# Batch norm with ReLU on one core: other roles for the two DMA queues, and stores of another size

## The chip, the cores and the metric

The kernel runs on one core of a Trainium2 chip. The metric is the device time of one execution in microseconds.

## The reference

```python
x = randn(32, 128, 32, 32)          # float32, 16.78 MB
normalized = (x - running_mean[None, :, None, None]) / sqrt(running_var[None, :, None, None] + eps)
scaled = normalized * gamma[None, :, None, None] + beta[None, :, None, None]
out = maximum(scaled, 0)            # float32, 16.78 MB
```

Per channel this is one scale, one bias and a ReLU. All 33.56 MB must pass between HBM (the memory beside the chip's cores, where the arrays lie) and SBUF (the core's own memory, on which the engines work).

## The kernel before

The 4096 (batch, channel) rows of 1024 numbers are laid out as two halves t, each of 128 partitions with 16 rows j. A row is 4 KB, and the rows of one partition are contiguous in HBM. `TILES` lists tiles as (half, first row, end row). A transfer of n rows is, for each partition, one contiguous run of n x 4 KB.

```python
TILES = ((0, 0, 2), (0, 2, 4), (0, 4, 8), (0, 8, 16), (1, 0, 16))
LOAD_CUTS = {(1, 8)}
STORE_CUTS = {(0, 1)}
HALVES = {(0, 0), (0, 1)}
# ...
for t, a, b in TILES:                                   # all loads: sync queue
    xt = data.tile([P, b - a, HW], F32, name=f"x{t}_{a}")
    cuts = [a] + [j for j in range(a + 1, b) if (t, j) in LOAD_CUTS] + [b]
    for c, d in zip(cuts, cuts[1:]):
        nc.sync.dma_start(out=xt[:, c - a : d - a, :], in_=xr[t, :, c:d, :])
# ...
for k, src in enumerate((running_var, gamma, running_mean, beta)):
    nc.scalar.dma_start(out=raw[:, k, :], in_=src.rearrange("(q j) -> q j", j=J))
# ... a matmul spreads the parameters over 128 partitions; Sqrt, reciprocal and
# ... three small VectorE operations make scale_t and bias_t
for t, a, b, xt in tiles:
    first = a
    for j in range(a, b):
        step = HW // 2 if (t, j) in HALVES else HW
        for w in range(0, HW, step):
            nc.scalar.activation(out=xt[:, j - a, w : w + step], in_=xt[:, j - a, w : w + step],
                                 func=ACTF.Relu, bias=bias_t[:, j : j + 1], scale=scale_t[:, j : j + 1])
        if j + 1 == b or (t, j + 1) in STORE_CUTS:      # all stores: scalar queue
            nc.scalar.dma_start(out=outr[t, :, first : j + 1, :], in_=xt[:, first - a : j + 1 - a, :])
            first = j + 1
```

## Time and profile before

| | before |
|---|---|
| time, median of the first 3 runs | 83.82 us (83.80 to 83.85) |
| span in the profile | 82.0 us |
| ScalarE busy | 39.1 us |
| the two DMA queues, of 16 engines' span | 48.7% + 47.6% |
| first packet of x / last packet | 1.80 / 80.81 us |
| last load landed / last ReLU ended | 46.84 / 56.0 us |

The share of the 16 DMA engines is best read by stage, in windows. One more source is used throughout: the trace's own record of each DMA packet, with queue, start, time and size. Views of the profile give sums of these; where single packets matter I counted them from the records. Two words: the ring of an issuing engine is its queue of packets at the DMA engines (q1 for sync, q10 for scalar), and a transfer has landed when its completion is signalled, after its last data packet.

### The profile page before, as it was taken

The numbers are of one execution on the slowest core, as the hardware profiler recorded it, in microseconds if no ns is written. First come the engines' busy times: TensorE is split into PE (matmuls) and PEld (weight loads), VectorE is DVE, ScalarE is ACT, GpSimd is POOL, SyncE is SP. The second block draws the span as 40 slices with busy tenths as digits, with TensorE's granted clock in tenths as the row PEclk, the third lists the DMA queues.
The fourth block names the chain that finished last, engine by engine and source line by source line (L and its number), as shares of the span: only waits on it lengthen the run. The fifth ranks groups of instructions, "written<-read, shape, count | busy, mean of one in ns | idle before, by whom it ended". The sixth has DMA issues, their size and how long they took to land.

```text
span 82.0 us, 120 instructions
## 1 busy us (share of the span) xinstructions
PE 0.7 (1%) x2; PEld 0.5 (1%) x2; DVE 0.8 (1%) x5; ACT 39.1 (48%) x36; POOL 0.8 (1%) x6
## 2 busy tenths in 40 slices
PE   0002000000000000000000000000000000000000
PEld 0002000000000000000000000000000000000000
DVE  0000300000000000000000000000000000000000
ACT  0600477799239999199994199993000000000000
POOL 3000000000000000000000000000000000000000
DMA  2899997979899989999799799998992999996590
GB/s 48 336 424 456 416 544 336 524 322 526 338 434 430 506 358 506 390 434 444 320 460 500 316 424 448 512 432 368 480 736 128 416 512 512 512 512 288 224 512 0
DMA packets 1792, 33.56 MB, mean 409 GB/s; under 512 B 256, under 2 KB 256, under 8 KB 512
## 3 DMA queue, kind: packets, MB, share of 16 engines
q1 hardware_dynamic: 864, 16.78, 48.7%
q10 hardware_dynamic: 928, 16.78, 47.6%
HBM read 16.78 MB, written 16.78 MB: 409 GB/s over the span
## 4 chain that ended last, share of the span: by engine, by line
DMA 56%; ACT 10%; issue 2%; SPq 0%
DMA x<-in_x_dram 56%; ACT x L102 10%; SPq L56 0%
## 5 line engine op out<-in xcount | busy, mean ns | idle before, releaser
L102 ACT ACTIVATE x<-x,bias_t,scale_t 128x1024 f32<-128x1024 f32 (+1 forms) x34 | 37.5, 1177 | 9.9 <-DMA x<-in_x_dram 7.6
L86 ACT ACT_TABLE_LOAD x1 | 1.3, 1283 | 2.6 <-issue 2.6
L86 ACT ACTIVATE std_t<-cols,eps_t 128x16 f32<-128x16 f32 x1 | 0.3, 273 | 4.5 <-PE cols L78 4.5
L78 PE MATMUL cols<-raw,rep 8*128 8x64 f32 x2 | 0.7, 429 | 7.6 <-DMA raw<-in_beta_dram 7.6
L78 PEld LDWEIGHTS cols<-raw,rep 8*128 8x128 f32 x2 | 0.5, 306 | 7.6 <-issue 7.6
L68 POOL TENSOR_SCALAR_AFFINE_SELECT rep<-rep 8x128 f32<-8x128 f32 x1 | 0.4, 392 | 0.1
L88 DVE RECIPROCAL rstd_t<-std_t 128x16 f32<-128x16 f32 x1 | 0.3, 254 | 7.7 <-ACT std_t L86 7.7
L67 POOL MEMSET rep<- 8x128 f32 x1 | 0.2, 194 | 0.3 <-POOLq L130 0.3
L90 DVE TENSOR_TENSOR scale_t<-cols,rstd_t 128x16 f32<-128x16 f32 x1 | 0.2, 175 | 0.1
L92 DVE TENSOR_TENSOR ms_t<-cols,scale_t 128x16 f32<-128x16 f32 x1 | 0.2, 175 | 0.0
L94 DVE TENSOR_TENSOR bias_t<-cols,ms_t 128x16 f32<-128x16 f32 x1 | 0.2, 174 | 0.0
L130 POOL MEMSET const-bfloat16-1.0<- 128x1 bf16 x1 | 0.1, 106 | 0.0
L130 POOL MEMSET const-uint8-127<- 128x1 uint8 x1 | 0.1, 106 | 0.0
L130 POOL MEMSET const-float32-0.0<- 128x1 f32 x1 | 0.1, 103 | 0.3 <-issue 0.3
L130 POOL MEMSET const-float32-1.0<- 128x1 f32 x1 | 0.1, 103 | 0.0
L65 DVE MEMSET eps_t<- 128x1 f32 x1 | 0.1, 59 | 0.9 <-PEq L130 0.9
## 6 DMA issues: line engine op xcount, KB each, us to landing
x<-in_x_dram SPq DMA_DIRECT2D x3, 4096.0 KB, 38.7
out_dram<-x ACTq DMA_DIRECT2D x1, 4096.0 KB, 28.7
x<-in_x_dram SPq DMA_DIRECT2D x2, 1024.0 KB, 5.8
x<-in_x_dram SPq DMA_DIRECT2D x1, 2048.0 KB, 11.3
out_dram<-x ACTq DMA_DIRECT2D x1, 2048.0 KB
out_dram<-x ACTq DMA_DIRECT2D x2, 512.0 KB, 19.6
out_dram<-x ACTq DMA_DIRECT2D x1, 1024.0 KB
raw<-in_running_var_dram ACTq DMA_DIRECT2D x1, 0.5 KB
```

Source lines behind the costliest of these rows:

```text
L65: nc.vector.memset(eps_t, float(eps))
L67: nc.gpsimd.memset(rep, 1.0)
L68: nc.gpsimd.affine_select(out=rep, in_=rep, compare_op=mybir.AluOpType.is_equal, fill=0.0, base=0, pattern=[[0, P // Q], [-1, Q]], channel ...
L78: nc.tensor.matmul(cols.rearrange("p k j -> p (k j)"), rep.rearrange("q r s -> q (r s)"), raw.rearrange("q k j -> q (k j)"), start=True, s ...
L86: nc.scalar.activation(out=std_t, in_=cols[:, 0, :], func=ACTF.Sqrt, bias=eps_t[:, 0:1], scale=1.0)
L88: nc.vector.reciprocal(out=rstd_t, in_=std_t)
L90: nc.vector.tensor_mul(out=scale_t, in0=cols[:, 1, :], in1=rstd_t)
L92: nc.vector.tensor_mul(out=ms_t, in0=cols[:, 2, :], in1=scale_t)
L94: nc.vector.tensor_sub(out=bias_t, in0=cols[:, 3, :], in1=ms_t)
L102: nc.scalar.activation(out=xt[:, j - a, w : w + step], in_=xt[:, j - a, w : w + step], func=ACTF.Relu, bias=bias_t[:, j : j + 1], scale=sc ...
L130: nc = _bacc.Bacc("TRN2", target_bir_lowering=False, num_devices=1)
```

## The change

The intent is to free ScalarE of issuing stores, to start with one 2 MB load of 4 rows, and to feed the first stores in four pieces of one row. The sync queue gets that first load and all stores; the scalar queue gets the parameters and the other loads, the last two of them placed behind the first and second ReLU in ScalarE's program (it issued them at 10.6 and 11.0 us, without waiting for a ReLU to end). A first Sqrt brings the table load forward.

```diff
-TILES = ((0, 0, 2), (0, 2, 4), (0, 4, 8), (0, 8, 16), (1, 0, 16))
+TILES = ((0, 0, 4), (0, 4, 16), (1, 0, 16))
-LOAD_CUTS = {(1, 8)}
-STORE_CUTS = {(0, 1)}
-HALVES = {(0, 0), (0, 1)}
+LOAD_CUTS = {(0, 8), (1, 8)}
+STORE_CUTS = {(0, 1), (0, 2), (0, 3)}
+LATE = 2
 ...
-            nc.sync.dma_start(out=xt[:, c - a : d - a, :], in_=xr[t, :, c:d, :])
+            loads.append((xt[:, c - a : d - a, :], xr[t, :, c:d, :]))
 ...
+        nc.sync.dma_start(out=loads[0][0], in_=loads[0][1])
+        for k, src in enumerate((running_var, gamma, running_mean, beta)):
+            nc.scalar.dma_start(out=raw[:, k, :], in_=src.rearrange("(q j) -> q j", j=J))
+        for dst, src in loads[1 : len(loads) - LATE]:
+            nc.scalar.dma_start(out=dst, in_=src)
+        nc.scalar.activation(out=first_t, in_=eps_t, func=ACTF.Sqrt)
 ... (ReLU: whole rows only)
-                    nc.scalar.dma_start(
+                    nc.sync.dma_start(
                         out=outr[t, :, first : j + 1, :], in_=xt[:, first - a : j + 1 - a, :]
                     )
+                for dst, src in [next(late)] if (t, j) < (0, LATE) else []:
+                    nc.scalar.dma_start(out=dst, in_=src)
```

More of the change, by code (lines that the diff above doesn't have):

```diff
@@ L51 @@
     tiles = []
+    loads = []
     for t, a, b in TILES:
@@ L55 @@
         for c, d in zip(cuts, cuts[1:]):
-            nc.sync.dma_start(out=xt[:, c - a : d - a, :], in_=xr[t, :, c:d, :])
+            loads.append((xt[:, c - a : d - a, :], xr[t, :, c:d, :]))
         tiles.append((t, a, b, xt))
     raw = params.tile([Q, 4, J], F32, name="raw")
-    for k, src in enumerate((running_var, gamma, running_mean, beta)):
-        nc.scalar.dma_start(out=raw[:, k, :], in_=src.rearrange("(q j) -> q j", j=J))
     eps_t = params.tile([P, 1], F32, name="eps_t")
     nc.vector.memset(eps_t, float(eps))
+    first_t = params.tile([P, 1], F32, name="first_t")
+    with tc.manual_schedule(engines={mybir.EngineType.Activation, mybir.EngineType.SP}):
+        nc.sync.dma_start(out=loads[0][0], in_=loads[0][1])
[4 more added lines that the diff above has]
+        nc.scalar.activation(out=first_t, in_=eps_t, func=ACTF.Sqrt)
     rep = params.tile([Q, P // Q, Q], F32, name="rep")
@@ L94 @@
     nc.vector.tensor_sub(out=bias_t, in0=cols[:, 3, :], in1=ms_t)
-    with tc.manual_schedule(engines={mybir.EngineType.Activation}):
+    late = iter(loads[len(loads) - LATE :])
+    with tc.manual_schedule(engines={mybir.EngineType.Activation, mybir.EngineType.SP}):
         for t, a, b, xt in tiles:
@@ L99 @@
             for j in range(a, b):
-                step = HW // 2 if (t, j) in HALVES else HW
-                for w in range(0, HW, step):
-                    nc.scalar.activation(
-                        out=xt[:, j - a, w : w + step],
-                        in_=xt[:, j - a, w : w + step],
-                        func=ACTF.Relu,
-                        bias=bias_t[:, j : j + 1],
-                        scale=scale_t[:, j : j + 1],
-                    )
+                nc.scalar.activation(
+                    out=xt[:, j - a, :],
+                    in_=xt[:, j - a, :],
+                    func=ACTF.Relu,
+                    bias=bias_t[:, j : j + 1],
+                    scale=scale_t[:, j : j + 1],
+                )
                 if j + 1 == b or (t, j + 1) in STORE_CUTS:
-                    nc.scalar.dma_start(
+                    nc.sync.dma_start(
                         out=outr[t, :, first : j + 1, :], in_=xt[:, first - a : j + 1 - a, :]
```

## The prediction

> **What bounds the kernel now.** I read the page from the top: engine shares first, then the DMA row of the 40 slices, then the queues.
>
> ```profile
> PE 0.7 (1%) x2; PEld 0.5 (1%) x2; DVE 0.8 (1%) x5; ACT 39.1 (48%) x36; POOL 0.8 (1%) x6
> ...
> DMA  2899997979899989999799799998992999996590
> ...
> q1 hardware_dynamic: 864, 16.78, 48.7%
> q10 hardware_dynamic: 928, 16.78, 47.6%
> ```
>
> The busiest compute engine, ScalarE, works 48% of the span. The two DMA queues together occupy 48.7 + 47.6 = 96.3% of what 16 DMA engines could give in 82.0 us, that is 79.0 us. q1 carries the loads (issued by the sync engine), q10 the stores and the four parameters (issued by ScalarE). Dips in the slice row could be real or an artefact of long packets booked in one slice, so I cut the span at the events that matter and asked for windows (columns: window, its length, busy us per engine, clock, DMA share, GB/s):
>
> ```profile
> 0.00:1.80 1.80, 0.00 (x0) 0.00 (x0) 0.06 (x1) 0.00 (x0) 0.80 (x6) 1.00 0.00 0
> 1.80:11.20 9.40, 0.66 (x2) 0.50 (x2) 0.78 (x4) 3.07 (x4) 0.00 (x0) 1.00 1.03 415
> 11.20:33.10 21.90, 0.00 (x0) 0.00 (x0) 0.00 (x0) 17.68 (x16) 0.00 (x0) 1.00 1.03 437
> 33.10:46.80 13.70, 0.00 (x0) 0.00 (x0) 0.00 (x0) 9.16 (x8) 0.00 (x0) 1.00 0.96 406
> 46.80:56.10 9.30, 0.00 (x0) 0.00 (x0) 0.00 (x0) 9.16 (x8) 0.00 (x0) 1.00 1.01 435
> 56.10:80.80 24.70, 0.00 (x0) 0.00 (x0) 0.00 (x0) 0.00 (x0) 0.00 (x0) 1.00 0.98 425
> 80.80:82.00 1.20, 0.00 (x0) 0.00 (x0) 0.00 (x0) 0.00 (x0) 0.00 (x0) 1.00 0.00 0
> ```
>
> From 1.8 to 80.8 us the share is about 1.0 in every stage, whether loads run alone, mixed with stores, or stores alone; only the first 1.8 and last 1.2 us carry nothing. The individual packet records agree: counted per microsecond, all 16 engines are occupied from 3 us to 80 us. **The DMA engines are the bound**, and their work is fixed: 33.56 MB. The chain of waits says the same less directly (56% waiting for a load), and would mislead if read as "loads are late": the last load landed at 46.84 us, the last ReLU ended near 56.0, and the stores already queued kept the engines busy beyond that.
>
> What one packet costs I took from the packet records, in median time by size: 4 KB 158 ns, 8 KB 309, 16 KB 611, 32 KB 1213, 64 KB 2418. That is 0.0368 ns per byte and some 8 ns per packet. A packet is the contiguous run of a partition: the rows of one transfer times 4 KB. One engine moves 33.56 MB / 16 = 2.097 MB: 77.1 us for bytes, and 96 data packets x 8 ns = 0.8 us. The remaining 1.1 us of the 79.0 is 0.5 us of slower packets before 3 us and about 0.5 us spread over 10 to 50 us.
>
> **What the Trainium skill says.** "DMA: Bandwidth & Descriptors", section "Issuing engines are not separate DMA queues": transfers issued by the sync and scalar engines end up on the same 16 DMA engines and interleave, so that choosing the issuer saves only issue time. The trace agrees: two rings, one sum of 96.3%. Same page, "Where 436 GB/s comes from": a fabric ceiling of 435 GB/s; the windows show 435 (46.8 to 56.1) and, averaged over 79.0 us, 33.56 MB / 79.0 = 425 GB/s. Same page, "Queues, rings and completion order": each DMA engine takes turns between rings, a packet at a time. The trace agrees in a way that matters here: the first two stores, one row each, have sixteen 4 KB packets per engine, and they take from 14.6 to 35.7 us, about 1.3 us each, which is one 4 KB plus one 32 KB load packet (158 + 1213 = 1371 ns). A small-packet store beside a large-packet load thus gets 4/36 of the bytes, not half.
>
> **The change part by part.**
>
> 1. Issue of stores moves off ScalarE. These are six issues of 0.34 to 0.37 us with a gap of about 0.45 us each:
>
> ```profile
> 9.61 1.52 ACT L102 ACTIVATE x<-x,bias_t,scale_t 128x512 f32<-128x512 f32 x2 [1.02 <-DVE bias_t L94]
> 11.16 0.37 ACTq L110 DMA_DIRECT2D out_dram<-x  x1
> ...
> 23.91 9.16 ACT L102 ACTIVATE x<-x,bias_t,scale_t 128x1024 f32<-128x1024 f32 x8 [2.94 <-DMA x<-in_x_dram]
> 33.10 0.34 ACTq L110 DMA_DIRECT2D out_dram<-x  x1
> 34.85 9.16 ACT L102 ACTIVATE x<-x,bias_t,scale_t 128x1024 f32<-128x1024 f32 x8 [1.78 <-DMA x<-in_x_dram]
> 46.87 9.16 ACT L102 ACTIVATE x<-x,bias_t,scale_t 128x1024 f32<-128x1024 f32 x8 [2.86 <-DMA x<-in_x_dram]
> 56.05 0.34 ACTq L110 DMA_DIRECT2D out_dram<-x  x1
> ```
>
> ScalarE already waits 1.8 to 2.9 us for each later load, so the saving, at most 6 x 0.45 = 2.7 us, falls into its idle time. Worth 0 to the end. Likewise the four half-row activations (805 ns mean) become two whole ones (1227): 0.8 us of ScalarE, not on the path. The early Sqrt brings forward a table load (1283 ns) that already ran at 2.57 us, long before the parameters landed at about 7.6. Worth 0.
>
> 2. The first load still leaves on the sync queue as its first instruction, at 0.81 us, with its first packet at 1.80. Start of the transfer: unchanged. It is now one 2 MB transfer in place of two of 1 MB, in 16 KB packets. In the kernel before these same bytes had landed at 8.10 us and the last parameter near 7.5. The parameter packets take turns with packets of 611 ns and not 309. From the first parameter that was held up (landed 6.2) to the last (7.5) they took two steps of 0.65 us, two packets each; doubled that would be 1.3 us more. But the first load's ring is empty after 8 packets per engine, about 1.8 + 8 x 0.611 + 0.5 = 7.2 us, so the delay is cut to about 0.5. First ReLU at 9.6 to 10.2 instead of 9.61. This costs nothing as long as the load ring is full, and it is: loads (0,4:8) and (0,8:16) come right behind the parameters and, with the first 2 MB, last 8.4 MB / 0.43 MB per us = 19.5 us, to about 21 us. The two late loads go out after the first and second ReLU, near 11 and 12.5 us, ample time ahead.
>
> 3. The order of the stores. Four one-row stores (32 packets of 4 KB per engine) stand ahead of a 6 MB store (0,4:16) in 48 KB packets, and an 8 MB one in 64 KB packets. Here lies the only danger. After the last load lands, eight ReLUs (9.16 us) must run before the last store can go, and the engines need queued stores to bridge that. By the turn-taking: at 14.6 us about 2 of the 24 load packets of 32 KB are done. The other 22 pair with 4 KB stores: 22 x 1.371 = 30.2, so loads end at 44.8 and land at about 45.4 (46.84 before). 32 - 22 = 10 small store packets are left, 1.6 us, and all of the 6 MB store, issued near 33: 8 x (49152 B x 0.0368 + 8) = 8 x 1.817 = 14.5 us. The backlog ends at 44.8 + 16.1 = 60.9. The last ReLU ends at 45.4 + 9.2 = 54.6, and its store's packets come about 1.0 us later (issue to first packet of the first load), 55.6. Margin: 5.3 us. So no gap.
>
> 4. Sum. Bytes unchanged; 88 data packets per engine instead of 96: 8 x 8 ns = -0.06 us. First packets larger, perhaps -0.1 of the 0.5 us at the start, which I count half. Work ends about 80.7 instead of 80.8, and span 81.9. Measured time is 1.8 us over the span (83.82 against 82.0): 83.7 us.
>
> **Rivals.** A: the small stores drain early. If the two rings shared by bytes and not by packets, the 2 MB of small stores would be out by about 25 us, the 6 MB store would run beside the loads, and the loads would end near 58 us with only about 2 us of stores left: a gap of 7 us or more, time 90 to 92. The 21 us that two small stores took now speaks against it; I give it 2 to 3%. B: ScalarE becomes the bound, as it now issues loads and a blocked issue would hold the ReLUs. Against it: only two loads are issued among the ReLUs, each about 0.4 us, and it has over 40 us of idle time. It would cost 0 to 1 us. C: the change helps more, because freed stores and one packet stream less remove the 0.5 us of slow packets in 10 to 50 us. At most 0.6 us in all, so 83.1: still within 2%. Even with perfect packets from 1.80 us on, 77.1 + 0.7 saves only 1.2 us, so over 2% faster would need an earlier start, which nothing here gives.
>
> **Range and chances.** Centre 83.7. Down to 83.2 if C holds, up to 84.3 if a wait of the sync engine or the parameters opens a small hole. Within 2% is 82.1 to 85.5.
>
> **What the changed profile should show.** DMA share about 1.0 from 1.8 to near 80.7; the first ReLU between 9.4 and 10.5; the last load landed at 45 to 46; 4 KB packets spread until the loads end and only then 48 KB ones; ScalarE busy about 38 us with longer waits for loads. Wrong if the DMA share drops between the last load's landing and the last store, or if 48 KB packets start before 44 us.

## The result, and the profile after

| | runs | median | range |
|---|---|---|---|
| before | 6 | 83.83 us | 83.80 to 83.94 |
| changed | 6 | 83.87 us | 83.73 to 83.99 |

The ratio is 1.0001, 95% interval 0.9987 to 1.0014: the same. A ratio here is the mean time of one kernel's fast runs over that of the other's fast runs of the same rounds, so it is not quite the ratio of the medians.

First the page of the changed kernel: busy times, and the DMA queues (packets, MB, share of 16 engines' span).

```profile
PE 0.7 (1%) x2; PEld 0.5 (1%) x2; DVE 0.8 (1%) x5; ACT 38.4 (47%) x35; POOL 0.8 (1%) x6
...
q1 hardware_dynamic: 1008, 18.87, 54.1%
q10 hardware_dynamic: 640, 14.68, 42.1%
```

The queues have exchanged cargo: q1 (sync) now moves the 16.78 MB of stores and 2.1 MB of loads. Their sum is 96.2%, where it was 96.3%. ScalarE has 0.7 us less to do, and nothing came of it.

Next the windows of the changed kernel, cut at its own events (first packet, last load, last ReLU, last packet); after the engines come clock, DMA share and GB/s:

```profile
0.00:1.80 1.80, 0.00 (x0) 0.00 (x0) 0.06 (x1) 0.00 (x0) 0.79 (x6) 1.00 0.00 0
1.80:11.20 9.40, 0.65 (x2) 0.49 (x2) 0.78 (x4) 2.35 (x4) 0.00 (x0) 1.00 1.03 413
11.20:33.10 21.90, 0.00 (x0) 0.00 (x0) 0.00 (x0) 17.73 (x16) 0.00 (x0) 1.00 1.02 436
33.10:46.00 12.90, 0.00 (x0) 0.00 (x0) 0.00 (x0) 9.16 (x8) 0.00 (x0) 1.00 0.95 394
46.00:55.20 9.20, 0.00 (x0) 0.00 (x0) 0.00 (x0) 9.15 (x8) 0.00 (x0) 1.00 1.08 467
55.20:81.00 25.80, 0.00 (x0) 0.00 (x0) 0.00 (x0) 0.01 (x1) 0.00 (x0) 1.00 0.96 417
81.00:82.20 1.20, 0.00 (x0) 0.00 (x0) 0.00 (x0) 0.00 (x0) 0.00 (x0) 1.00 0.00 0
```

The share stays about 1.0 from 1.8 to 81.0 us. A share a little under or over 1 is a long packet booked in one window and running on in the next; counted packet by packet, all engines are occupied in each microsecond from 3 to 80.

Last the timeline of the changed kernel (start, duration, engine, line, what; in brackets the idle time before and what ended it):

```profile
10.61 1.24 ACT L111 ACTIVATE x<-x,bias_t,scale_t 128x1024 f32<-128x1024 f32 x1 [1.02 <-DVE bias_t L104]
10.62 0.82 ACTq L124 DMA_DIRECT2D x<-in_x_dram  x2
11.76 8.01 ACT L111 ACTIVATE x<-x,bias_t,scale_t 128x1024 f32<-128x1024 f32 x7
11.88 43.68 SPq L119 DMA_DIRECT2D out_dram<-x  x6
23.63 9.16 ACT L111 ACTIVATE x<-x,bias_t,scale_t 128x1024 f32<-128x1024 f32 x8 [3.86 <-DMA x<-in_x_dram]
34.56 9.16 ACT L111 ACTIVATE x<-x,bias_t,scale_t 128x1024 f32<-128x1024 f32 x8 [1.78 <-DMA x<-in_x_dram]
46.05 9.16 ACT L111 ACTIVATE x<-x,bias_t,scale_t 128x1024 f32<-128x1024 f32 x8 [2.33 <-DMA x<-in_x_dram]
```

The stores and their gaps of 0.45 us are gone from ScalarE, and what was saved bought nothing: the wait before 23.63 us is 3.86 where it was 2.94 (the three waits for loads together 8.0 us, where they were 7.6), and the first ReLU starts at 10.61, a microsecond later than before (9.61), which is swallowed too.

### The profile page after: what moved, and what is told of

It is laid out like the page before. It is cut to its first block, busy times and chain, and to the rows that moved or that the text cites. A ratio compares the mean times of both kernels' runs of the same rounds, so it can differ in the third digit from the quotient of the medians.

```text
span 82.2 us, 120 instructions
## 1 busy us (share of the span) xinstructions
PE 0.7 (1%) x2; PEld 0.5 (1%) x2; DVE 0.8 (1%) x5; ACT 38.4 (47%) x35; POOL 0.8 (1%) x6
## 2 busy tenths in 40 slices
DMA packets 1648, 33.56 MB, mean 408 GB/s; under 512 B 240, under 2 KB 240, under 8 KB 752
## 3 DMA queue, kind: packets, MB, share of 16 engines
HBM read 16.78 MB, written 16.78 MB: 408 GB/s over the span
## 4 chain that ended last, share of the span: by engine, by line
DMA 50%; ACT 11%; ACTq 3%; DVE 1%; PE 1%; issue 1%; DVEq 0%
DMA x<-in_x_dram 43%; ACT x L111 10%; DMA raw<-in_beta_dram 8%; ACTq L71 1%; ACTq L155 1%; PE cols L88 1%; ACT std_t L96 0%; DVE rstd_t L98 0%; DVE bias_t L104 0%; DVE ms_t L102 0%; DVE scale_t L100 0%; DVEq L100 0%
## 5 line engine op out<-in xcount | busy, mean ns | idle before, releaser
L111 ACT ACTIVATE x<-x,bias_t,scale_t 128x1024 f32<-128x1024 f32 x32 | 36.6, 1227 | 9.0 <-DMA x<-in_x_dram 8.0
## 6 DMA issues: line engine op xcount, KB each, us to landing
x<-in_x_dram ACTq DMA_DIRECT2D x1, 2048.0 KB, 10.5
```

Of the source, the lines that this page charges most:

```text
L111: nc.scalar.activation(out=xt[:, j - a, :], in_=xt[:, j - a, :], func=ACTF.Relu, bias=bias_t[:, j : j + 1], scale=scale_t[:, j : j + 1],)
```

## The experiments

The experiments ran on three chips: the first four on one, the next four (from "The changed kernel again" on) on another, called the second chip below, and the last three on the third chip. "First chip" is that of the first measurement. Each call timed the kernel before as well; times of different calls are compared by their ratios to it.

The theory: the 16 DMA engines are full from first to last packet and set the time; they take turns between the two rings packet by packet, whatever the packet's size, so the small packets of the four one-row stores hold back the stores until the loads are through. The rivals: queue roles matter by themselves; ScalarE was on the path; sizes do not matter because bytes are the same.

**Roles put back.** The cuts stay, the queues change back.

```diff
-LATE = 2
+LATE = 0
-            nc.scalar.dma_start(out=dst, in_=src)      # loads
+            nc.sync.dma_start(out=dst, in_=src)
-                    nc.sync.dma_start(                 # stores
+                    nc.scalar.dma_start(
```

> The changed kernel with the roles of the queues as before: all loads on the sync queue (none of them late), stores on the scalar queue; the cuts stay. Theory (the 16 DMA engines are full, and take turns between the rings by packet whoever issued them): 83.8 to 83.9 us, ratio to the kernel before 0.998 to 1.003, the same order of packets: 4 KB stores paired with 32 KB loads until about 45.5 us. Rival (issue or the ring that a transfer is on matters): over 0.5 us away from 83.87 in either direction.

Measured: 84.03 us against 83.65 for the kernel before on this chip, ratio 1.0041 (1.0023 to 1.0058). The packets are as in the changed kernel: 4 KB ones from 15.7 to 47.0 us, the last 32 KB load packet ended at 45.3. The ratio missed the stated 0.998 to 1.003, but the changed kernel itself came out at 1.0035 and 1.0037 on the next two chips (below). Set beside those, the roles by themselves are worth nothing that these runs can see. This compares ratios from different chips.

**One 2 MB store instead of four small ones.**

```diff
-STORE_CUTS = {(0, 1), (0, 2), (0, 3)}
+STORE_CUTS = set()
```

> The changed kernel with one 2 MB store of 4 rows (16 KB packets) in place of four one-row stores. Theory (turns by packet: the 4 KB packets held the stores back): the 16 KB packets pair with 32 KB loads (1.82 us a pair) and are out by about 33 us, the 48 KB packets of the 6 MB store then pair with the last 8 or 9 loads (3.03 us a pair), the last load ends near 60.6 us and lands near 61, nothing is queued while 8 ReLUs run (9.2 us plus issue), so a hole of about 10.9 us: span near 92 us, time 93 to 95 us. Rival 1 (rings share by bytes): a hole of about 8 us, time 90 to 92. Rival 2 (size of stores does not matter, as bytes are the same): 83.9 us.

Measured: 99.22 us, ratio 1.1849 (1.1818 to 1.1880). A single change of cut, same bytes, same queues, costs 15 us. Windows, then two lines of the timeline, of this run:

```profile
33.00:38.40 5.40, 0.00 (x0) 0.00 (x0) 0.00 (x0) 1.85 (x3) 0.00 (x0) 1.00 0.92 397
38.40:66.20 27.80, 0.00 (x0) 0.00 (x0) 0.00 (x0) 8.95 (x8) 0.00 (x0) 1.00 0.93 357
66.20:76.40 10.20, 0.00 (x0) 0.00 (x0) 0.00 (x0) 9.16 (x8) 0.00 (x0) 1.00 0.00 0
```

```profile
38.19 9.16 ACT L111 ACTIVATE x<-x,bias_t,scale_t 128x1024 f32<-128x1024 f32 x8 [3.55 <-DMA x<-in_x_dram]
66.49 9.16 ACT L111 ACTIVATE x<-x,bias_t,scale_t 128x1024 f32<-128x1024 f32 x8 [19.14 <-DMA x<-in_x_dram]
```

The hole is there: from 66.2 to 76.4 us no byte moves while eight ReLUs run. The last load, at 46.0 us in the changed kernel, landed at 66.5 here, because the 6 MB store's 48 KB packets took their turns beside it. The small store was out at 33.0 us, as worked out. But the time is 4 us over the top of the expected range. Two terms were missing. Packets were slow: the busy time per engine is 82.2 us, 3.1 more than in the changed kernel, mostly while 48 KB and 32 KB packets alternate (48 KB took 2084 ns in the median, 1815 elsewhere). And a load's four-byte completion packet waits its turn too: the last load's data ended at 64.3 us, the last completion packets started at 66.1, behind 48 KB store packets. So between first and last packet an engine was idle for 12.0 us in the mean (0.03 in the changed kernel), where a hole of 10.9 had been worked out. The changed kernel's 83.9, plus 3.1, plus 12.0, is 99.0.

**Two two-row stores.**

```diff
-STORE_CUTS = {(0, 1), (0, 2), (0, 3)}
+STORE_CUTS = {(0, 2)}
```

> The changed kernel with two two-row stores (8 KB packets) in place of four one-row stores. Theory (turns by packet): 16 pairs of 1.52 us, small stores out near 40 us, about 5 load packets left to pair with 48 KB ones (3.03 us), last load ends near 55 us, the 48 KB packets near 61, last ReLU near 65, hole about 5 us: time 88 to 90.5 us. Rival 1 (shares by bytes): as with one store, 90 to 92. Rival 2 (size does not matter): 83.9 us.

Measured: 89.15 us, ratio 1.0659 (1.0633 to 1.0685). Windows of this run:

```profile
39.80:56.10 16.30, 0.00 (x0) 0.00 (x0) 0.00 (x0) 6.15 (x6) 0.00 (x0) 1.00 1.04 450
56.10:61.50 5.40, 0.00 (x0) 0.00 (x0) 0.00 (x0) 5.05 (x5) 0.00 (x0) 1.00 0.67 291
61.50:66.40 4.90, 0.00 (x0) 0.00 (x0) 0.00 (x0) 4.10 (x4) 0.00 (x0) 1.00 0.00 0
```

Small packets out at 39.7 us (expected near 40), last load packet ended at 54.2 (55), 48 KB packets out at 61.5 (61), hole of 4.9 us (5). With packets of 4, 8 and 16 KB for the same 2 MB, the hole is 0, 4.9 and 10.2 us: the size of a packet decides how fast a store drains beside loads. A division by bytes would have given 90 to 92 for both sizes, and no effect of size would have given 83.9; both rivals fall. That 48 KB beside 32 KB was slow for one store but not here (1815 ns throughout) stays unexplained.

**More work for ScalarE.** The 16 rows of the first half in half-row activations.

```diff
+                step = HW // 2 if t == 0 else HW
+                for w in range(0, HW, step):
-                    out=xt[:, j - a, :], in_=xt[:, j - a, :],
+                        out=xt[:, j - a, w : w + step], in_=xt[:, j - a, w : w + step],
 ... (lines joined; the rest of the call is as it was)
```

> The changed kernel with ScalarE given more work: the 16 rows of the first half in half-row activations (805 ns each, 1.61 us a row in place of 1.15 to 1.23), some 6 to 7 us more in all. Theory (ScalarE has slack, only the DMA engines bound the time): ScalarE busy 44 to 46 us in place of 38.4, time 83.8 to 83.95 us, ratio to before within 0.3% of 1. Rival (ScalarE is on the path, so freeing it of the stores should have gained): 1 us or more longer.

Measured: 84.13 us, ratio 1.0051 (1.0033 to 1.0069). The page of this run:

```profile
PE 0.7 (1%) x2; PEld 0.5 (1%) x2; DVE 0.8 (1%) x5; ACT 42.7 (52%) x51; POOL 0.8 (1%) x6
```

ScalarE did 4.3 us more; I had reckoned 6 to 7, since half rows in a train followed each other every 0.71 us (15 in 10.66 us) and not every 0.805. The ratio again missed the stated 0.3%; beside 1.0035 and 1.0037 of the unedited changed kernel, at most some 0.15% (0.1 us) remains, within the intervals, for 4.3 us of added work. ScalarE is not on the path.

**The changed kernel again.** Both ratios above needed this.

> The changed kernel itself, on the same chip as the next three, since the kernel before came out 0.2 us faster on the chip of the first experiments than on that of the first measurement. Theory: ratio to before 1.000 to 1.005, so that the 1.0041 of the roles put back and the 1.0051 of the added ScalarE work are the changed kernel's own ratio on such a chip. Rival (those two edits cost something): ratio within 0.0015 of 1, as in the first measurement.

Measured: 83.90 us against 83.53, ratio 1.0035 (1.0014 to 1.0056). So on this chip, the second, the changed kernel is a little slower than the one before.

**One ring.** Loads on the sync queue as well, all ahead of the stores.

```diff
-LATE = 2
+LATE = 0
-            nc.scalar.dma_start(out=dst, in_=src)      # loads
+            nc.sync.dma_start(out=dst, in_=src)
```

> The changed kernel with the loads on the sync queue as well, so that loads and stores share one ring, all loads ahead of all stores; only the parameters stay on the scalar queue. Theory (the engines are full with one ring as with two, in order of issue): no pairing at all, 4 KB packets only after the last load, last load ends near 41.3 us, small stores near 46.4, 48 KB near 61, end near 80.5; time 83.3 to 83.9 us. If mixing of loads and stores is what makes some packets slower between 10 and 50 us, up to 0.4 us are gained. Rival (two rings are needed to fill the engines): DMA share below 1 and over 1 us longer.

Measured: 84.59 us, ratio 1.0115 (1.0095 to 1.0135), 0.7 us over the changed kernel of the same call. Windows of this run:

```profile
1.80:38.60 36.80, 0.65 (x2) 0.49 (x2) 0.77 (x4) 26.22 (x25) 0.00 (x0) 1.00 1.01 427
38.60:42.80 4.20, 0.00 (x0) 0.00 (x0) 0.00 (x0) 3.01 (x3) 0.00 (x0) 1.00 0.93 276
42.80:81.60 38.80, 0.00 (x0) 0.00 (x0) 0.00 (x0) 9.16 (x8) 0.00 (x0) 1.00 1.00 430
```

One ring fills the engines; 4 KB packets come only from 42.3 us. But I had guessed that mixing loads and stores makes slow packets and that a clean cut would save up to 0.4 us. Half of this held: from 5 to 36 us, unmixed, not one packet was slow, where the changed kernel lost 0.2 to 0.4 us per engine (table below). But then the last two 32 KB load packets of each engine, from 38.7 us on, took up to 2153 ns in place of 1213. Shortly before the ring passes from loads to stores, 1.2 us per engine are lost at once; with two rings, smaller losses are spread over several places. The gain that I guessed, and with it the range of 83.3 to 83.9 us, is refuted; what inside the engine causes the loss, the trace does not say.

**First load in 8 KB packets.**

```diff
-TILES = ((0, 0, 4), (0, 4, 16), (1, 0, 16))
+TILES = ((0, 0, 2), (0, 2, 4), (0, 4, 16), (1, 0, 16))
-        nc.sync.dma_start(out=loads[0][0], in_=loads[0][1])
+        for dst, src in loads[:2]:
+            nc.sync.dma_start(out=dst, in_=src)
 ...
-        for dst, src in loads[1 : len(loads) - LATE]:
+        for dst, src in loads[2 : len(loads) - LATE]:
```

> The changed kernel with its first 2 MB loaded as two transfers of two rows (8 KB packets), as in the kernel before. Theory (the last parameter lands later because its packets take turns with 16 KB packets): parameters land near 7.5 us in place of 8.5, first ReLU near 9.6 in place of 10.6, time unchanged: within 0.15 us of the changed kernel of this call. Rival 1 (the delay comes from the loads that follow on the parameters' ring): first ReLU stays near 10.6. Rival 2 (an earlier first ReLU shortens the whole): time falls by 0.5 to 1 us.

Measured: 84.15 us, ratio 1.0063 (1.0043 to 1.0082). Timeline of this run:

```profile
7.46 0.65 PE L89 MATMUL cols<-raw,rep 8*128 8x64 f32 x2 [7.46 <-DMA raw<-in_beta_dram]
...
9.45 1.24 ACT L112 ACTIVATE x<-x,bias_t,scale_t 128x1024 f32<-128x1024 f32 x1 [1.02 <-DVE bias_t L105]
```

The parameters landed a microsecond earlier and the first ReLU began at 9.45 us: the delay did come from turns with 16 KB packets. It did not shorten anything. The time rose by 0.25 us over the changed kernel of this call, more than the 0.15 I had allowed; the slow packets at the end of the loads were worse in this trace (0.65 us against 0.09), for which I have no cause.

**Fewer, larger packets on one ring.** A try at beating both.

```diff
-TILES = ((0, 0, 4), (0, 4, 16), (1, 0, 16))
+TILES = ((0, 0, 16), (1, 0, 16))
-STORE_CUTS = {(0, 1), (0, 2), (0, 3)}
+STORE_CUTS = set()
 (and the edits of one ring)
```

> One ring as in the run above, with fewer and larger packets: loads of 8 rows (32 KB) and two stores of 16 rows (64 KB), 48 data packets per engine in place of 88. Theory (8 ns per packet, and no mixing): 0.3 us less than the run of one ring, 83.0 to 83.6 us; the backlog holds (first store issued near 32, last ReLU near 51, first store ends near 60.5). Rival (what is left is not in packets): as the run of one ring within 0.1 us.

Measured: 84.63 us, ratio 1.0113 (1.0089 to 1.0137), not different from one ring. The busy time per engine did fall, from 79.73 to 79.45 us, as 40 packets fewer at some 8 ns require. But first start plus busy time is 1.83 + 79.45 = 81.28 us and the last packet ended at 81.81, so engines stood idle for 0.5 us on average; on one ring it was 81.55 and 81.61. What fewer packets gave was lost to engines that did not finish together: their last packets ended at 81.28 in the mean and at 81.81 the latest, on one ring at 81.43 and 81.61. The 1.2 us before the first stores came again.

**The kernel before, the changed one and a graded one, on a third chip.** The graded one stores rows 0 and 1 singly and rows 2 and 3 as one.

```diff
-STORE_CUTS = {(0, 1), (0, 2), (0, 3)}
+STORE_CUTS = {(0, 1), (0, 2)}
```

> The kernel before against itself, for its trace on the same chip as the next two. Ratio within 0.2% of 1. On the chip of the first measurement the changed kernel was equal (1.0001), on that of the second call 0.35% slower (1.0035). Theory: the difference lies in how many slow packets the end of the loads and the first stores bring, not in a hole: busy time of the 16 engines near 79.0 us or a little less, no idle engine from 3 to 80 us.

> The changed kernel on the same chip. Ratio to before between 0.999 and 1.006. If the small difference is real and is due to slow packets, the busy time of the 16 engines is larger than that of the kernel before by about what the time is, 0.1 to 0.3 us; if it is due to anything else (start, end), busy times are equal.

> The changed kernel with rows 2 and 3 in one two-row store, so that the small stores are graded (two of 4 KB packets, one of 8 KB) as in the kernel before. Theory of turns: 16 pairs of 1.371 us, then about 5 pairs of 1.522 us, loads end near 45.3 us as in the changed kernel, only 2 to 4 of the 8 KB packets are left then, the backlog still lasts to about 61, no hole: 83.6 to 84.0 us. Theory that slow load packets at the end of the loads come from the small stores: their excess there falls from 0.12 to 0.4 us to about 0.1. Rival: the margin is thinner than worked out and a hole opens, time over 84.5 us.

Measured: before 83.69 us, ratio 1.0004 to itself (0.9983 to 1.0024); changed 83.94, ratio 1.0037 (1.0020 to 1.0055); graded 83.94, ratio 1.0042 (1.0019 to 1.0065). From the packet records, per DMA engine in us; "slow" is what packets took over 0.0368 ns per byte and 8.5 ns each:

| trace | busy in all | slow, to 5 us | slow, 5 to 36 | slow, 36 to 50 | packets x 8.5 ns |
|---|---|---|---|---|---|
| before, first chip | 78.99 | 0.47 | 0.28 | 0.18 | 0.82 |
| before, third chip | 78.76 | 0.37 | 0.24 | 0.09 | 0.82 |
| changed, first chip | 79.16 | 0.60 | 0.18 | 0.38 | 0.75 |
| changed, second chip | 79.08 | 0.56 | 0.44 | 0.09 | 0.75 |
| changed, third chip | 79.11 | 0.56 | 0.30 | 0.26 | 0.75 |
| graded, third chip | 79.06 | 0.53 | 0.28 | 0.33 | 0.68 |
| first load in 8 KB | 79.27 | 0.39 | 0.16 | 0.65 | 0.82 |
| one ring | 79.73 | 0.54 | 0.00 | 1.20 | 0.75 |

On the third chip the changed kernel's engines are busy 0.35 us longer and its runs take 0.25 us longer: the small difference seems to lie in slow packets. This is one trace of each, and the two traces of the kernel before differ by 0.23 us in busy time between themselves, so it is indicated and not proved. About 0.1 to 0.2 us of it is the start, where the size of the first packets is the likely reason: 0.37 to 0.47 us in the three traces with 8 KB, 0.53 to 0.60 in the five here with 16 KB (of the runs with 16 KB that are not in the table, the one with half rows showed 0.45, the others 0.61 to 0.70). The rest, at the end of the loads, varies from trace to trace. Grading the stores did not lower it (0.33), and it was largest on one ring, where no small store ran beside a load; nothing supports the theory that the small stores cause it. No hole opened in the graded run. No version tried beats the kernel before.

## Why the prediction was right

*The bound.* Right, and shown: share about 1.0 from first to last packet in both kernels. Moving 4.3 us of work onto ScalarE did nothing to speak of, putting the roles back neither, and any hole among the packets showed at once in the time.

*Step 1, ScalarE freed.* Right: 38.4 us busy where about 38 was said, and nothing gained at the end. Of the three waits for loads only the first is longer (3.86 us; then 1.78 as before, and 2.33 where it was 2.86).

*Step 2, the start.* The mechanism was right and the size was off. The parameters' delay was to be cut to about 0.5 us because the first load's ring would be empty at 7.2 us; the first ReLU was to come at 9.6 to 10.2 (10.5 at most) and came at 10.61. That 7.2 was right where it counts. The records carry no engine number, but each parameter comes in eight packets, and those of the last one (7.25 to 7.68) follow within 0.01 us on eight completion packets of the first load (7.24 to 7.67): on these engines its ring was empty by then. (The other eight completions come at 8.58 and later; there the first load took turns with the next load, which delays no parameter.) The last parameter's packets came 0.6 us later than before (7.69, where it was 7.08), about the 0.5 that was said. The term that was left out is the time from there to the landing: 0.8 us (8.49), where it was 0.4 (7.49). Why that grew, no run shows. With first packets of 8 KB both parts of the delay vanished (6.96, landed 7.33).

*Step 3, the order of the stores.* Right to about a microsecond: last load landed at 46.02 (45.4, and "45 to 46"), 4 KB packets until 47.2 (46.4), last ReLU 55.2 (54.6), 48 KB packets from 46.8 to 61.7 (60.9). The sum took the start of the pairs, 14.6 us, from the kernel before; here they began at 15.8, with the same 2 load packets per engine done. The last store was issued at 55.23 and, with 1.0 us to its first packet, had 5.4 us in hand (5.3). Rival A had only the old trace against it at the time; the stores of 16 KB and 8 KB packets then showed what it fears, a hole of 10.2 and 4.9 us, and for the reason given, turns by packet.

*Step 4, the sum.* Within the range, with a small term of the wrong sign. "First packets larger, perhaps -0.1" measured +0.1 to +0.2, and work ended at 81.00, not 80.7. In the first measurement this does not show (1.0001); on two other chips it does, as 0.35 to 0.37%. Why the first chip shows less stays open: the traces of that chip differ by 0.17 us of busy time. The 1.8 us that the sum adds to the span sets the median of three runs beside the profile of a run that took 83.68; each profile against its own run gives 1.7, before and after. Rival C, that less mixing would gain, failed: slow packets from 5 to 50 us cost 0.56 us in the changed kernel, where they cost 0.46, and the run of one ring lost more. Rival B cost nothing.

## What to carry to other kernels

Where, as here, the DMA engines are full from first packet to last, rearranging issuers gains nothing; look for the holes instead, and ask what is queued while the last compute runs. In these traces the engines share by packets and not by bytes, so the length of the contiguous run is a throttle: short runs for early stores beside long runs for loads leave the stores queued until they are needed, and here one changed cut was worth 15 us. Before shortening a list of small stores, work out the pairs (each small packet takes a small plus a large packet's time while loads run): what is still queued when the loads end must outlast the last compute and the issue of its store. Here that was some 16 us of packets (45.5 to 61.7) against 10.7 (45.5 to about 56.2).

## What the Trainium skill lacked or had wrong

- "DMA: Bandwidth & Descriptors", Queues, rings and completion order: it has the round-robin by packet, with packets of some 9 to 17 descriptors, but not what follows from it. In these records a packet is one contiguous run of 4 to 64 KB, 4 KB and 32 KB alternate one for one (1371 ns a pair), and packets of 4, 8 or 16 KB for the same 2 MB store made a hole of 0, 4.9 and 10.2 us.
- The same page, Rules for kernel authors: that spreading transfers over issuing engines does not help bandwidth holds here in the main, since one ring also fills the engines (share 0.93 to 1.01 by window). It has, in another row, that two rings interleave by packet, but not what the order of packets can be worth: all on one ring took 84.59 us, two rings 83.90 on the same chip.
- The same page, Where 436 GB/s comes from: its sentence that the HBM side, about 358 GB/s, binds transfers between HBM and SBUF does not hold for this one core: 33.56 MB (half read, half written) in 79.0 us are 425 GB/s, with the engines full. (The page's own single-core measurement says 425 too.)
- No page that I read has the slow packets shortly before a stream of loads passes into stores: 1.2 us per engine on one ring, the last 32 KB loads taking up to 2153 ns in place of 1213.
- "DMA: Bandwidth & Descriptors", Latency and other measured facts, has some 600 ns to the first byte on this path, and does not say from when it counts. Here it was 1.0 us from the start of the first load's issue (0.81) to its first packet (1.80), but 0.6 us from the end of that issue (1.19), which agrees.
